# The feed-forward of a two-layer flow trunk: gate and up by seven products of halves, then the down product

## The chip, the cores and the metric

The kernel runs on one core of one Trainium2 chip. The metric is the device time of one execution in microseconds; of the kernel before three timed runs are shown, with a median of 3389.33 us (3386.82 to 3394.78).

## The reference

A trunk of two layers over 1024 latent tokens (`x`) with 256 context tokens (`ctx`), model width D = 1024, all in float32. A layer mixes tokens (gating, windowed attention, a recurrence) and then runs the feed-forward, which is the part that the change touches. Cut to that:

```python
D_FF = 2816                       # 22 blocks of 128

def swiglu(h, w_gu, w_down):
    gu = h @ w_gu                 # 1024 -> 2 * 2816: gate and up
    return (jax.nn.silu(gu[..., :D_FF]) * gu[..., D_FF:]) @ w_down

def trunk_layer(x, xc, c_act, cc_act, lp, last):
    sh1, sc1, gt1, sh2, sc2, gt2 = split(c_act @ lp['w_mod'] + lp['b_mod'], 6)   # modulations
    ...
    h = modulate(rms_norm(x, g[2]), sh2, sc2)
    x = x + gt2 * rms_norm(swiglu(h, lp['w_gu'], lp['w_down']), g[3])
    if last:
        return x, xc
    hc = modulate(rms_norm(xc, g[2]), mc[3], mc[4])
    xc = xc + mc[5] * rms_norm(swiglu(hc, lp['w_gu'], lp['w_down']), g[3])
```

So layer 0 sends 1024 latents and 256 context tokens through the feed-forward, layer 1 the 1024 latents alone.

## The kernel before

**Number format.** Products are made in three passes: each operand is split into hi (ScalarE copy to fp32r) and lo (VectorE, value minus hi), and `mm3` (L147) issues hi x hi, hi x lo and lo x hi into the same PSUM accumulator. All its matmuls stand in line L145. Weights come from DRAM in float32 as 128 x 1024 (512 KB) and are split on chip: `emit_w` loads into one of two buffers `wr` (L221), splits on ACT into `wh` (L229) and on DVE into `wl` (L230); `wh` and `wl` share six buffers. Which weights are loaded, and in which order, is the list `plan`, filled ahead; `wget` hands out the next pair and keeps two ready.

**Tokens.** They are in three groups `TG`: 0 = the 256 context columns, 1 and 2 = 512 latent columns each. The input of the feed-forward is transposed, `h2[z][k]`: z is hi or lo, k one of 8 blocks of 128 model columns, 1280 token columns in a slot. There are 33 such slots (`alloc`, `rel`); PSUM has accumulators `mm` (2 of one bank), `xx` (2 of one bank) and `dd` (2 of two banks).

**The feed-forward (from L1503).** For each block f of 128 hidden columns `gate_up(f)` runs `gu_group` for each token group: gate into the first bank of a `dd` accumulator, up into the second, each over 8 k. Then comes silu(gate) x up: tanh on ACT (L1518), two DVE operations (L1519, L1520), and the split of the result into `ah` (ACT, L1522) and `al` (DVE, L1523), which stay in slots. After each pair of f, `ffn_down` multiplies them by `w_down`: for each tile of 128 tokens and each half of 512 output columns a product of the two f into `mm` or `xx`, added by DVE to `yac`, the sum in SBUF (L1550):

```python
        ffn_down((0,), [wget()], True)
        gate_up(2)
        for q in range(NQ):
            ...
            gate_up(2 * q + 3, mq(0))
            ffn_down((2 * q + 1, 2 * q + 2), [wget(), wget()], False)
            gate_up(2 * q + 4, mq(1))
        gate_up(NFF - 1)
```

The first two f are interleaved with the norm that makes `h2`; the last call of `ffn_down` takes three f and calls `finish` for each tile: norm, residual and store. In layer 0, `mods_quarter` computes three of the modulations of layer 1 beside gate and up: 48 loads of `w_mod` into slots `wm`, two to a step, and 192 matmuls of 32 x 512. POOL has no work in the feed-forward.

Engines run their own instructions in the order in which the program issued them; they wait for one another through semaphores that the framework sets. All the loads and stores named here are issued by SP.

Of the kernel before, what the change touches and what calls it, by code (L numbers as in the profile page):

```python
# [17 lines left out]
L = 2  # L18
DM = 1024
# [16 lines left out]
FA = 6, 7, 8, 9  # L36
NP = 2
PPW = 111
C_DECAY = 0.3032653298563167
# [52 lines left out]
def trunk(ctx: ExitStack, tc: tile.TileContext, x, ctxt, cc, w_mod, pp, w_in, w_out, lng, lnb, sgw, sink,  # L92
# [50 lines left out]

    def mm(o, lhsT, rhs, start=True, stop=True):
        T.matmul(o, lhsT=lhsT, rhs=rhs, start=start, stop=stop)  # L145

    def mm3(o, a, b, start, stop):  # L147
        mm(o, a[0], b[0], start, False)
        mm(o, a[0], b[1], False, False)
        mm(o, a[1], b[0], False, stop)  # L150

# [83 lines left out]
    def wget(ahead=2, slots=False):  # L235
        if not ready:
            emit_w(slots)
        r = ready.popleft()
        while len(ready) < ahead and plan:
            emit_w(slots)  # L240
        return r
# [25 lines left out]

    NQ = (NFF - 4) // 2
    for k in range(8):
# [3 lines left out]
    for l in range(L):  # L273
        for n, i in enumerate(MIXT):
            plan_in(l, mix_col(i), 128)
            if l == 0:
                for _ in range(MODN[n]):
                    plan.extend(mblk.popleft())
        for c0 in (256, 0, OFF_CTX, OFF_Q, OFF_Q + 256):
            plan_in(l, c0, 256)  # L280
        for k in range(8):
            plan_rows(w_out[l], k)
        if l == 0:
            for k in range(8):
                plan.extend(mod_blocks(0, 2, k))
        plan_gu(l, 0)
        plan_gu(l, 1)
        plan_rows(w_down[l], 0)
        plan_gu(l, 2)
        for q in range(NQ):  # L290
            plan_gu(l, 2 * q + 3)
            if l + 1 < L and q < 6:
                for k in range(2):
                    plan.extend(mod_blocks(l + 1, q // 2, 4 * (q % 2) + k))
            plan_rows(w_down[l], 2 * q + 1)
            plan_rows(w_down[l], 2 * q + 2)
            plan_gu(l, 2 * q + 4)
            if l + 1 < L and q < 6:
                for k in range(2, 4):
                    plan.extend(mod_blocks(l + 1, q // 2, 4 * (q % 2) + k))  # L300
        plan_gu(l, NFF - 1)
        for f in range(NFF - 3, NFF):
            plan_rows(w_down[l], f)

# [12 lines left out]

    def mod_step(ps, k, start, stop):


        w = wget(), wget()
# [13 lines left out]

    def mods(l, qs, bank=d_t):

        for q in qs:
            ps = bank()
            for k in range(8):  # L340
                mod_step(ps, k, k == 0, k == 7)
# [8 lines left out]
    def mods_quarter(l, q, g, acc):  # L350

        ps = x_t()
        for k in (2 * g, 2 * g + 1):
            mod_step(ps, k, k == 2 * g, k == 2 * g + 1)
            yield
        for z in range(2):
            c = ps[:, z * 256:(z + 1) * 256]
            if g == 0:
                S.activation(acc[z], c, AF.Copy)
            else:  # L360
                V.tensor_tensor(acc[z], acc[z], c, op=ALU.add)
        yield
        if g == 3:
            mod_cols(l, q, x_t(), lambda kk: acc[kk // 2][:, (kk % 2) * 128:(kk % 2) * 128 + 128])

# [50 lines left out]

    def norm_apply(l, which, gi, xn, hT):

        c0, n = TG[gi]
        strm = 1 if gi == 0 else 0  # L420
        for k2 in range(4):
            tmp = alloc("ntmp")
            for kk in range(2):
                ps = x_t() if kk else mm_t()
                k = 2 * k2 + kk
                for j, s in enumerate(xn):
# [4 lines left out]
                             bias=AB[l][:, 2 * which + 1, 2 * k + strm:2 * k + strm + 1])  # L431
                hi, lo = hk(hT, k, c0, n)
                if kk:
# [5 lines left out]
            if k2 == 3:  # L439
                rel(*xn)  # L440
            yield

    def g_tiles(gi):
# [114 lines left out]
    def layer(l):  # L558
# [943 lines left out]
        rel(lora, *GB.values(), *Y)  # L1502
        h2 = hT_alloc()  # L1503


        act = {}

        def gu_group(gi, w, ah, al, tmp):
            c0, n = TG[gi]
            ps = d_t()  # L1510
            for z in range(2):
                for k in range(8):
                    mm3(ps[:, z * 512:z * 512 + n], (w[z][0][:, k * 128:(k + 1) * 128], w[z][1][:, k * 128:(k + 1) * 128]),
                        hk(h2, k, c0, n), k == 0, k == 7)
                    if k % 4 == 3:
                        yield
            tm = tmp.t[:, c0:c0 + n]
            S.activation(tm, ps[:, 0:n], AF.Tanh, scale=0.5)  # L1518
            V.scalar_tensor_tensor(tm, tm, 1.0, ps[:, 0:n], op0=ALU.add, op1=ALU.mult)  # L1519
            V.tensor_tensor(tm, tm, ps[:, 512:512 + n], op=ALU.mult)  # L1520
            hi = ah.t[:, c0:c0 + n]
            S.activation(hi, tm, AF.Copy, scale=0.5)  # L1522
            V.scalar_tensor_tensor(al.t[:, c0:c0 + n], tm, 0.5, hi.bitcast(F32), op0=ALU.mult, op1=ALU.subtract)  # L1523

        def gate_up(f, mg=None):
            w = wget(), wget()
            ah, al = alloc("ah", F32R), alloc("al", F32R)
            tmp = alloc("ft")
            n = 0
            for gi in gord:  # L1530
                for _ in gu_group(gi, w, ah, al, tmp):
                    n += 1
                    if mg and n in (2, 5, 7, 9):
                        next(mg, None)
            rel(tmp)
            act[f] = (ah, al)

        def ffn_down(fs, wd_, first, after=None, order=gord, side=iter(())):
            pend = []
            for t in [t for gi in order for t in g_tiles(gi)]:  # L1540
                for h in range(2):
                    c = slice(h * 512, (h + 1) * 512)
                    ps = mm_t() if h == 0 else x_t()
                    for j, f in enumerate(fs):
                        a = tuple(s.t[:, t * 128:(t + 1) * 128] for s in act[f])
                        mm3(ps, a, tuple(w[:, c] for w in wd_[j][:2]), j == 0, j == len(fs) - 1)
                    if first:
                        S.activation(yac[t].t[:, c], ps, AF.Copy)
                    else:
                        V.tensor_tensor(yac[t].t[:, c], yac[t].t[:, c], ps, op=ALU.add)  # L1550
                if after:
                    pend.append(after(t))
                    for g in list(pend):
                        if next(g, pend) is pend:
                            pend.remove(g)
                    next(side, None)
            for f in fs:
                rel(*act.pop(f))
            for g in pend:
                run(g)  # L1560
# [28 lines left out]
        ft = alloc("ft")  # L1589
        ff = []  # L1590

        def n2(gi):
            n2_load(gi)
            yield from norm_apply(l, 1, gi, [keep[t] for t in g_tiles(gi)], h2)

        def gu2(gi):
            for f in range(2):
                if gi == gord[0]:
                    ff.append((alloc("ah", F32R), alloc("al", F32R)))
                yield from gu_group(gi, wf[f], *ff[f], ft)  # L1600

        run(n2(gord[0]))
        for i, gi in enumerate(gord):
            weave(gu2(gi), n2(gord[i + 1]) if i + 1 < len(gord) else iter(()))
        for f in range(2):
            rel(*[z for w in wf[f] for z in w[2]])
            act[f] = ff[f]
        rel(ft)
        yac = {t: alloc("yac") for t in tiles_q}
        macc = [yac[t].t[:, DM:NTOK] for t in tiles_q[:2]]  # L1610
        ffn_down((0,), [wget()], True)
        gate_up(2)
        for q in range(NQ):
            def mq(z):
                return mods_quarter(l + 1, q // 2, 2 * (q % 2) + z, macc) if not last and q < 6 else None
            gate_up(2 * q + 3, mq(0))
            ffn_down((2 * q + 1, 2 * q + 2), [wget(), wget()], False)
            gate_up(2 * q + 4, mq(1))
        gate_up(NFF - 1)
        rel(*h2[0], *h2[1])  # L1620
        wd_ = [wget(0), wget(0), wget()]
        for strm in ([1, 0] if full else [0]):
            GB[strm] = gb_tile(l, 1, strm)
        if last:
            ffn_down(tuple(range(NFF - 3, NFF)), wd_, False, finish)
        else:
# [13 lines left out]

            ffn_down(tuple(range(NFF - 3, NFF)), wd_, False, finish, (2, 1, 0), norm_late())
            hT.append(h_slots())
# [74 lines left out]
```

## Time and profile before

| | |
|---|---|
| median of 3 timed runs | 3389.33 us (3386.82 to 3394.78) |
| profiled execution | 3392.51 us, span 3390.7 us |
| PE (matmul) | 3274.7 us, 97%, 20,348 records |
| DVE | 1787.4 us, 53%, 3,747 instructions |
| ACT | 1254.8 us, 37%, 2,735 |
| POOL | 330.9 us, 10%, 464 |
| mean DMA rate | 105 GB/s |
| PE on the chain that ended last | 21% of the span is named there, nearly all of it L145 |

A busy share is the engine's busy time over the span. It counts time in which the engine was at work, not time in which another had to wait for it; for that there are the chain of waits, the windows and the idle time before each group of instructions. The span is the time from the first to the last record of the profiled execution, which itself lasted 1.8 us longer.

### The profile page before, as it was taken

The numbers are of one execution on the slowest core, as the hardware profiler recorded it, in microseconds if no ns is written. First come the engines' busy times: TensorE is split into PE (matmuls) and PEld (weight loads), VectorE is DVE, ScalarE is ACT, GpSimd is POOL, SyncE is SP. The second block draws the span as 40 slices with busy tenths as digits, with TensorE's granted clock in tenths as the row PEclk, the third lists the DMA queues.
The fourth block names the chain that finished last, engine by engine and source line by source line (L and its number), as shares of the span: only waits on it lengthen the run. The fifth ranks groups of instructions, "written<-read, shape, count | busy, mean of one in ns | idle before, by whom it ended". The sixth has DMA issues, their size and how long they took to land. (4 is left out here: it accounts for less than half of the span.)

```text
span 3390.7 us, 51725 instructions
## 1 busy us (share of the span) xinstructions
PE 3274.7 (97%) x20348; PEld 2659.0 (78%) x20348; DVE 1787.4 (53%) x3747; ACT 1254.8 (37%) x2735; POOL 330.9 (10%) x464
## 2 busy tenths in 40 slices
PE   7998999999999999999999998999999999999998
PEld 4777877777787777778888777877777788888887
DVE  3458769775423333333334657788675433433445
ACT  4354477664431111111112554477664411111112
POOL 2103101231100000000000213111221000000000
PEclk8898999999999999999999999999999999999999
DMA  5684322446412222222112375423445111111113
GB/s 208 224 252 140 91 62 67 137 135 211 155 32 81 87 81 71 73 87 63 38 38 87 111 235 176 128 57 96 111 126 208 56 44 50 50 50 50 50 43 119
DMA packets 381778, 354.38 MB, mean 105 GB/s; under 512 B 111968, under 2 KB 332768, under 8 KB 381536
## 3 DMA queue, kind: packets, MB, share of 16 engines
q1 hardware_dynamic: 381536, 351.09, 32.9%
q8 instruction: 160, 2.62, 0.3%
q14 instruction: 82, 0.67, 0.1%
HBM read 255.20 MB, written 95.81 MB: 104 GB/s over the span
## 5 line engine op out<-in xcount | busy, mean ns | idle before, releaser
L145 PE MATMUL dd<-h,wh 128*128 128x512 f32 (+1 forms) x3440 | 983.7, 370 | 2.8 <-DVE h L437 2.7
L145 PEld LDWEIGHTS dd<-h,wh 128*128 128x128 f32 x3440 | 624.8, 189 | 140.7 <-issue 30.2
L145 PE MATMUL dd<-h,wl 128*128 128x512 f32 (+1 forms) x1720 | 634.5, 369 | 0.0
L229 ACT ACTIVATE wh<-wr 128x1024 fp32r<-128x1024 f32 x172 | 180.7, 1058 | 677.1 <-PE xx L145 367.0
L230 DVE TENSOR_TENSOR wl<-wr,wh 128x1024 fp32r<-128x1024 f32 x172 | 209.5, 1225 | 342.7 <-ACT wh L229 338.1
L145 PEld LDWEIGHTS dd<-h,wl 128*128 128x128 f32 x1720 | 325.0, 189 | 58.6 <-issue 5.0
L145 PE MATMUL mm<-wh,h 128*128 128x256 f32 x1472 | 327.6, 299 | 0.0
L1519 DVE SCALAR_TENSOR_TENSOR ft<-ft,dd 128x512 f32<-128x512 f32 (+1 forms) x110 | 69.5, 632 | 455.6 <-ACT ft L1518 455.6
L145 PEld LDWEIGHTS mm<-wh,h 128*128 128x128 f32 x1472 | 252.6, 197 | 15.6 <-issue 14.6
L1518 ACT ACTIVATE ft<-dd 128x512 f32<-128x512 f32 (+1 forms) x110 | 60.5, 550 | 497.7 <-PE dd L145 497.1
L145 PE MATMUL mm<-h,wh 128*128 128x512 f32 (+1 forms) x816 | 236.7, 375 | 1.0 <-ACT ntmp L429 0.7
L177 POOL TENSOR_TENSOR ss<-ss,mh_sb 128x1 f32<-128x1 f32 x74 | 49.9, 676 | 1830.8 <-DVE ss L406 1824.6
L145 PE MATMUL mm<-wl,h 128*128 128x256 f32 x736 | 213.7, 290 | 4.7 <-DVE wl L230 4.7
L145 PEld LDWEIGHTS mm<-h,wh 128*128 128x128 f32 x816 | 147.7, 196 | 34.7 <-issue 10.8
L1550 DVE TENSOR_TENSOR yac<-yac,mm 128x512 f32<-128x512 f32 x180 | 123.4, 686 | 86.9 <-PE mm L145 86.9
L1550 DVE TENSOR_TENSOR yac<-yac,xx 128x512 f32<-128x512 f32 x180 | 123.4, 686 | 84.7 <-PE xx L145 84.7
L145 PE MATMUL mm<-wh,ah 128*128 128x512 f32 x396 | 155.3, 392 | 2.1 <-DVE yac L1550 1.9
L145 PE MATMUL mm<-wh,al 128*128 128x512 f32 x396 | 154.7, 391 | 0.0
L145 PE MATMUL xx<-wh,ah 128*128 128x512 f32 x396 | 154.7, 391 | 0.0
L145 PE MATMUL mm<-wl,ah 128*128 128x512 f32 x396 | 154.6, 390 | 0.0
L145 PE MATMUL xx<-wl,ah 128*128 128x512 f32 x396 | 154.1, 389 | 0.0
L145 PE MATMUL xx<-wh,al 128*128 128x512 f32 x396 | 154.1, 389 | 0.0
(316 smaller groups left out, 5958.0 us busy)
## 6 DMA issues: line engine op xcount, KB each, us to landing
wr<-in_w_gu SPq DMA_DIRECT2D x88, 512.0 KB, 3.7
wm<-in_w_mod SPq DMA_DIRECT2D x80, 512.0 KB, 4.6
wr<-in_w_down SPq DMA_DIRECT2D x44, 512.0 KB, 3.3
wr<-in_w_in SPq DMA_DIRECT2D x38, 512.0 KB, 4.8
cb<-ao SPq DMA_DIRECT2D x76, 256.0 KB, 3.2
ao<-rk SPq DMA_DIRECT2D x58, 256.0 KB, 4.1
xs<-xr SPq DMA_DIRECT2D x28, 512.0 KB, 2.7
xr<-xs SPq DMA_DIRECT2D x26, 512.0 KB, 4.3
```

What stands on the lines that cost most here:

```text
L145: T.matmul(o, lhsT=lhsT, rhs=rhs, start=start, stop=stop)
L177: G.tensor_tensor(dst, src, mh[:, :n], op=ALU.pow)
L229: S.activation(hi, raw, AF.Copy)
L230: V.tensor_tensor(lo, raw, hi.bitcast(F32), op=ALU.subtract)
L1518: S.activation(tm, ps[:, 0:n], AF.Tanh, scale=0.5)
L1519: V.scalar_tensor_tensor(tm, tm, 1.0, ps[:, 0:n], op0=ALU.add, op1=ALU.mult)
L1550: V.tensor_tensor(yac[t].t[:, c], yac[t].t[:, c], ps, op=ALU.add)
```

## The change

The feed-forward is cut into two phases. In the first all activations are made and stored to DRAM as float32 (`actd`, 128 x 1280 for each f); in the second they are loaded again, split and multiplied by `w_down`.

**Phase 1.** f = 0, 1, 2 (`NCL` = 3) are computed as before (`gu_group`), with a store in the place of the split (L1511). For f = 3 to 21 gate and up of the latents are made together by one level of the Winograd form of Strassen's products. The weight block is a 2 x 2 array (gate, up by the two halves of k), the activations a 2 x 2 array (halves of k by halves of the columns; `h2k` lays the columns so that a half is 512 contiguous columns, 256 of each token group). Seven products of 4 k x 3 passes stand for eight. The sums of weights are made for each f by POOL in `prep` (L1565 to 1569), from `g` and `u`, loaded one f ahead; the four matrices g, u, a, b are split on ACT and DVE (L1575, L1576), two of them in `prep`, two at the start of the products (`w.late`). The sums of activations T1 to T4 are made once per layer, beside f = 0 to 2, by `t_sums` and `t_last` (DVE and ACT). `visit` makes one f. The context columns (layer 0) are computed as before, inside the visit.

```diff
+        def visit(f, w, tmp, aux):
+            a, c, d = mm_t(), x_t(), d_t()
+            b = d[:, 0:512]
...
+            p1, q = aux.t[:, 0:512], aux.t[:, 512:1024]
...
+            w.late[0]()
+            prod(1, a, True)
+            ctx(d[:, 512:768], 0, 0, True, False)
+            yield
+            S.activation(p1, a, AF.Copy)
+            prod(6, b, True)
+            yield
+            V.tensor_tensor(h2_, v(p1), v(b), op=ALU.add)
+            prod(5, c, True)
+            w.late[1]()
+            yield
+            V.tensor_tensor(q, p1, c, op=ALU.add)
+            prod(2, a, False, True)
+            ctx(d[:, 512:768], 0, 4, False, True)
+            yield
+            S.activation(h1, v(a), AF.Tanh, scale=0.5)
+            V.scalar_tensor_tensor(h1, h1, 1.0, v(a), op0=ALU.add, op1=ALU.mult)
+            prod(7, b, False)
+            yield
+            V.tensor_tensor(q, q, b, op=ALU.add)
+            prod(3, c, False, True)
+            yield
+            V.tensor_tensor(v(c), h2_, v(c), op=ALU.add)
+            ctx(d[:, 768:1024], 1, 0, True, False)
+            ctx(d[:, 768:1024], 1, 4, False, True)
+            prod(4, b, False, True)
+            silu(h2_, v(c), v(q))
+            yield
...
+            V.tensor_tensor(p1, p1, b, op=ALU.add)
+            V.tensor_tensor(h1, h1, v(p1), op=ALU.mult)
+            if f < NFF - 1:
+                lo = 0 if full else 256
+                D.dma_start(actd[f][:, lo:], tmp.t[:, lo:])
```

In it `prod` issues the 12 matmuls of one product, onto accumulator a (`mm`), b (first bank of a `dd`) or c (`xx`); `h1`, `h2_` are the halves of one slot `tmp`, which is then stored (L1649); `tmp` and `aux` are the same two slots for all f.

```diff
+        def prep(f, side, own):
...
+            for z, t in enumerate((g, u)):
+                D.dma_start(t.rearrange("p (a b) -> p a b", a=8), wv[:, :, z * DFF + f * 128:z * DFF + (f + 1) * 128])
+            yield
...
+            G.tensor_tensor(a[:, 0:512], u[:, 0:512], u[:, 512:1024], op=ALU.add)
+            G.tensor_tensor(a[:, 512:1024], a[:, 0:512], g[:, 0:512], op=ALU.subtract)
+            yield
+            G.tensor_tensor(b[:, 0:512], g[:, 0:512], u[:, 0:512], op=ALU.subtract)
+            G.tensor_tensor(b[:, 512:1024], g[:, 512:1024], a[:, 512:1024], op=ALU.subtract)
```

**Phase 2.** `ffn_down` runs over 8 groups of f, where there were 11 calls. Beside each group the next one's raw activations and rows of `w_down` are loaded (`act_load`, `wd_load`) and split (`act_split` on L1663 and L1664, `wd_split` on L1680 and L1681), one step for each token tile. The weights of every second group go to slots, those of the others to the six `wh` buffers. In layer 0 one step of the modulations of layer 1 (`mods` with `mget`, two loads ahead) stands beside each tile from the second group on; `mods_quarter` is gone.

```diff
+DOWN = [(0, 21), (1, 2, 3), (4, 5, 6), (7, 8, 9), (10, 11, 12), (13, 14, 15), (16, 17), (18, 19, 20)]
...
+        for i, fs in enumerate(DOWN[:-1]):
+            new = DOWN[i + 1]
+            slots = i % 2 == 1
...
+            def beside():
+                g = loads()
+                while True:
+                    next(g, None)
+                    if i:
+                        next(mg, None)
+                    yield
```

**On PE, in layer 1.** Before, a stretch of gate and up: `dd` is one accumulator for 24 matmuls, `h` are hi and lo of the activations, `wh` and `wl` those of the weights.

```order
L145 MATMUL dd_28397<-h_24627,wl_28208 128x512
L145 MATMUL dd_28397<-h_24628,wh_28207 128x512 x2
L145 MATMUL dd_28397<-h_24628,wl_28208 128x512
L145 MATMUL dd_28397<-h_24629,wh_28207 128x512 x2
L145 MATMUL dd_28397<-h_24629,wl_28208 128x512
L145 MATMUL dd_28397<-h_24622,wh_28213 128x512 x2
L145 MATMUL dd_28397<-h_24622,wl_28214 128x512
```

Now, the end of product 3 (onto c, `xx`) and the beginning of product 4 (onto b, `dd`) of one visit:

```order
L147 MATMUL xx_25967<-h_24702,wl_25970 128x512
L147 MATMUL xx_25967<-h_24703,wh_25969 128x512
L147 MATMUL xx_25967<-h_24711,wh_25969 128x512
L147 MATMUL xx_25967<-h_24703,wl_25970 128x512
L147 MATMUL dd_25968<-h_24696,wh_26019 128x512 [waits DVE_49,Activation_49]
L147 MATMUL dd_25968<-h_24704,wh_26019 128x512
L147 MATMUL dd_25968<-h_24696,wl_26020 128x512
```

An accumulator is now written by one product, read by DVE, and written by a later product of the same visit; product 4 waits for DVE's reading of b (L1634).

**On DVE, in layer 1.** Before, the end of one token group, two splits of weights and the end of the next:

```order
L1519 SCALAR_TENSOR_TENSOR ft_28219<-ft_28219,dd_28220 128x512 [waits Activation_49]
L1520 TENSOR_TENSOR ft_28219<-ft_28219,dd_28220 128x512 [waits DVE_49]
L1523 SCALAR_TENSOR_TENSOR al_28218<-ft_28219,ah_28217 128x512 [waits Activation_49]
L230 TENSOR_TENSOR wl_28214<-wr_28211,wh_28213 128x1024 [waits DMAHW3_49,PE_49,Activation_49]
L230 TENSOR_TENSOR wl_28331<-wr_28328,wh_28330 128x1024 [waits DMAHW4_49,PE_49,Activation_49]
L1519 SCALAR_TENSOR_TENSOR ft_28219<-ft_28219,dd_28274 128x512 [waits Activation_49]
```

Now, one visit whole, from the first addition after product 6 to the split that stands ahead of the next visit's (`ft` is `tmp`, `aux` holds p1 and q, `wu` and `wq` the weight matrices):

```order
L1622 TENSOR_TENSOR ft_24737<-aux_25335,dd_25842 128x2x256 [waits DMAHW6_49,PE_49,Activation_49]
L1626 TENSOR_TENSOR aux_25335<-aux_25335,xx_25841 128x512 [waits PE_49]
L1576 TENSOR_TENSOR wl_25894<-wu_25734,wh_25893 128x1024 [waits DMAHW1_49,Activation_49]
L1576 TENSOR_TENSOR wl_25913<-wq_25859,wh_25912 128x1024 [waits DMAHW5_49,PE_49,Activation_49]
L1631 SCALAR_TENSOR_TENSOR ft_24737<-ft_24737,mm_25840 128x2x256 [waits Activation_49]
L1634 TENSOR_TENSOR aux_25335<-aux_25335,dd_25842 128x512 [waits DVE_49,PE_49]
L1637 TENSOR_TENSOR xx_25841<-ft_24737,xx_25841 128x512 [waits PE_49]
L1576 TENSOR_TENSOR wl_25931<-wq_25876,wh_25930 128x1024 [waits Activation_49]
L1495 SCALAR_TENSOR_TENSOR ft_24737<-ft_24737,xx_25841 128x2x256 [waits Activation_49]
L1645 TENSOR_TENSOR aux_25335<-aux_25335,dd_25842 128x512 [waits PE_49]
L1496 TENSOR_TENSOR ft_24737<-ft_24737,aux_25335 128x2x256 [waits DVE_49]
L1646 TENSOR_TENSOR ft_24737<-ft_24737,aux_25335 128x2x256 [waits DVE_49]
```

Each f had four additions and multiplications, two splits of weights and two of activations; it now has nine of the first kind (one of them the first row) and four splits of weights. The first row waits for a DMA: the store of the f before, out of the same slot.

**On SP, in layer 1.** Before, two f of gate and up and a pair of down:

```order
L221 DMA wr_27047<-in_w_gu 128x8x128 [waits DMAHW6_49,DVE_49]
L221 DMA wr_27053<-in_w_gu 128x8x128 [waits DMAHW7_49,DVE_49]
L221 DMA wr_27170<-in_w_down 128x1024 [waits DMAHW0_49,DVE_49]
L221 DMA wr_27176<-in_w_down 128x1024 [waits DMAHW1_49,DVE_49]
L221 DMA wr_27293<-in_w_gu 128x8x128 [waits DMAHW2_49,DVE_49]
L221 DMA wr_27299<-in_w_gu 128x8x128 [waits DMAHW3_49,DVE_49]
```

Now, three visits:

```order
L1562 DMA wu_25860<-in_w_gu 128x8x128 [waits DMAHW6_49,DVE_49]
L1562 DMA wq_25859<-in_w_gu 128x8x128 [waits DMAHW2_49,DMAHW5_49,DVE_49,Pool_49]
L1649 DMA actd_24712<-ft_24737 128x1024 [waits DVE_49]
L1562 DMA wu_25986<-in_w_gu 128x8x128 [waits DMAHW1_49,DVE_49]
L1562 DMA wq_25985<-in_w_gu 128x8x128 [waits DMAHW0_49,DMAHW5_49,DVE_49,Pool_49]
L1649 DMA actd_24712<-ft_24737 128x1024 [waits DVE_49]
```

The loads of g (`wq`) and u (`wu`) for f + 1 stand between the store of f - 1 and that of f (L1649); a store waits for DVE's last multiplication (L1646), and the loads behind it wait with it.

## Rows read from the trace of the kernel before

**Rows 1.** Page: span, busy time and share by engine, GB/s in 40 slices.
```profile
span 3390.7 us, 51725 instructions
...
PE 3274.7 (97%) x20348; PEld 2659.0 (78%) x20348; DVE 1787.4 (53%) x3747; ACT 1254.8 (37%) x2735; POOL 330.9 (10%) x464
...
GB/s 208 224 252 140 91 62 67 137 135 211 155 32 81 87 81 71 73 87 63 38 38 87 111 235 176 128 57 96 111 126 208 56 44 50 50 50 50 50 43 119
```

**Rows 2.** Windows: feed-forward of layer 0, of layer 1, and two f there.
```profile
core 0: us, PE busy (x) PEld busy (x) DVE busy (x) ACT busy (x) POOL busy (x), PEclk, DMA share, GB/s
943.50:1676.90 733.40, 729.02 (x3555) 584.16 (x3553) 252.41 (x372) 120.88 (x181) 0.00 (x0) 1.00 0.23 70
2670.30:3344.70 674.40, 674.40 (x2978) 558.37 (x2977) 255.88 (x337) 124.58 (x165) 0.00 (x0) 1.00 0.17 53
2713.60:2757.20 43.60, 43.60 (x194) 36.08 (x194) 11.02 (x13) 8.37 (x13) 0.00 (x0) 1.00 0.16 48
```

**Rows 3.** Chain by time, layer 1: start us, us, engine, tile, line, count.
```profile
3170.77 43.52 PE dd L145 x192
3214.29 1.36 PE mm L145 x6
3215.65 1.36 PE xx L145 x6
```

**Rows 4.** Timeline of PE, layer 0: start us, us; context columns, then modulation.
```profile
start us, us, engine line op out<-in xcount [idle before <-releaser]
...
1108.64 0.28 PE L145 MATMUL dd<-h,wl 128*128 128x256 f32 x1
...
1111.52 0.28 PE L145 MATMUL dd<-h,wl 128*128 128x256 f32 x1
1112.52 1.05 PE L145 MATMUL xx<-wm,c 128*32 128x512 f32 x4 [0.72 <-DMA wm<-in_w_mod]
```

**Rows 5.** Groups of DVE and ACT, shapes apart: | busy us, mean ns |.
```profile
L230 DVE TENSOR_TENSOR wl<-wr,wh 128x1024 fp32r<-128x1024 f32 x172 | 209.5, 1225 | 342.7 <-ACT wh L229 338.1 <-PE mm L467 4.2 <-PE mm L145 0.4
...
L1550 DVE TENSOR_TENSOR yac<-yac,mm 128x512 f32<-128x512 f32 x180 | 123.4, 686 | 86.9 <-PE mm L145 86.9
...
L1523 DVE SCALAR_TENSOR_TENSOR al<-ft,ah 128x512 fp32r<-128x512 f32 x88 | 60.8, 691 | 47.9 <-ACT ah L1522 47.8
...
L1520 DVE TENSOR_TENSOR ft<-ft,dd 128x512 f32<-128x512 f32 x88 | 60.3, 685 | 2.3
...
L970 DVE TENSOR_TENSOR q<-mm,rope 128x256 f32<-128x256 f32 x32 | 13.4, 419 | 7.9 <-PE mm L145 7.5
...
L229 ACT ACTIVATE wh<-wr 128x1024 fp32r<-128x1024 f32 x172 | 180.7, 1058 | 677.1 <-PE xx L145 367.0 <-PE dd L145 269.7 <-PE mm L145 32.2
...
L1522 ACT ACTIVATE ah<-ft 128x512 fp32r<-128x512 f32 x88 | 55.6, 632 | 154.9 <-DVE ft L1520 154.9
...
L1518 ACT ACTIVATE ft<-dd 128x512 f32<-128x512 f32 x88 | 52.0, 591 | 387.5 <-PE dd L145 387.5
```

**Rows 6.** Groups of POOL, shapes apart: additions of 512 columns.
```profile
L437 POOL TENSOR_TENSOR h<-ntmp,h 128x512 fp32r<-128x512 f32 x16 | 21.7, 1358 | 58.2 <-DVE h L436 32.9 <-ACT h L434 16.0 <-ACT yt L400 5.7
...
L1326 POOL TENSOR_TENSOR gsx<-gsx,gkr 128x512 f32<-128x512 f32 x8 | 10.4, 1299 | 23.6 <-ACT gsx L1324 17.3 <-DMA gkr<-rk 6.3
```

**Rows 7.** Timeline of DVE and POOL, two places: start us, us.
```profile
922.20 1.29 POOL L437 TENSOR_TENSOR h<-ntmp,h 128x512 fp32r<-128x512 f32 x1 [9.35 <-DVE h L436]
922.21 1.82 DVE L437 TENSOR_TENSOR h<-ntmp,h 128x512 fp32r<-128x512 f32 x1
...
2546.84 1.28 POOL L1336 TENSOR_TENSOR Y<-Y,gsx 128x512 f32<-128x512 f32 x1 [6.70 <-DVE gsx L1335]
...
2547.03 2.16 DVE L230 TENSOR_TENSOR wsl<-wr,wsh 128x1024 fp32r<-128x1024 f32 x1
```

**Rows 8.** DMA issues: count, KB each, median us to landing.
```profile
wr<-in_w_gu SPq DMA_DIRECT2D x88, 512.0 KB, 3.7
...
wm<-in_w_mod SPq DMA_DIRECT2D x80, 512.0 KB, 4.6
...
wraw<-in_w_mod SPq DMA_DIRECT2D x16, 512.0 KB, 10.4
```

**Rows 9.** Line L1461, stores of 512 KB to DRAM.
```profile
DMA to landing us min/median/max: 2.6/2.8/5.1
```

**Rows 10.** Groups, layer 0: modulation matmuls, idle time and its releaser.
```profile
L145 PE MATMUL xx<-wm,c 128*32 128x512 f32 x192 | 44.3, 604 | 4.4 <-DMA wm<-in_w_mod 4.4
```

More of the change, by code (lines that the diff above doesn't have):

```diff
@@ L238, in wget @@
         r = ready.popleft()
-        while len(ready) < ahead and plan:
+        while len(ready) < ahead and plan and plan[0]:
             emit_w(slots)
@@ L285, in trunk @@
                 plan.extend(mod_blocks(0, 2, k))
[L286 to L303, printed above, removed]
+        for f in range(NCL):
+            plan_gu(l, f)
+        plan.append(None)
     S.activation(sc_, CC, AF.Tanh, scale=0.5)
@@ L1517, in gu_group @@
             tm = tmp.t[:, c0:c0 + n]
[L1518 to L1536, printed above, removed]
@@ L1539, in ffn_down, with wd_split @@
+        def wd_split(w):
+            hi, lo, own, raw = w
+            S.activation(hi, raw, AF.Copy)
+            V.tensor_tensor(lo, raw, f32(hi), op=ALU.subtract)
+        def ffn_down(fs, wd_, first, after=None, order=None, side=iter(())):
             pend = []
-            for t in [t for gi in order for t in g_tiles(gi)]:
+            for t in order:
                 for h in range(2):
@@ L1619, in layer, with both, sums @@
-        gate_up(NFF - 1)
-        rel(*h2[0], *h2[1])
-        wd_ = [wget(0), wget(0), wget()]
+                yield from gu_group(f, gi, wf[f], ft)
+        def both(*gs):
+            for g in gs:
+                yield from g
+        def sums(gi, kks):
+            for kk in kks:
+                if kk not in TT:
+                    TT[kk] = [alloc("tt", F32R) for _ in range(3)]
+                    if kk % 2 == 0:
+                        T4[kk // 2] = alloc("t4")
+                yield from t_sums(gi, kk)
@@ new lines, in layer, with plain @@
+        run(n2(gord[0]))
+        for i, gi in enumerate(gord[:-2]):
+            weave(gu2(gi), n2(gord[i + 1]))
+        ga, gb = gord[-2:]
+        weave(gu2(ga), both(n2(gb), sums(ga, (0, 1))))
+        side = []
+        more = [(wget(0), wget(0)) for _ in range(2, NCL)]
+        own = []
+        nxt = prep(NCL, side, own)
+        def plain(f):
+            w = more.pop(0)
+            for gi in gord:
+                yield from gu_group(f, gi, w, ft)
+            rel(*[z for x in w for z in x[2]])
@@ new lines, in after_two @@
+        def after_two():
+            yield from gu2(gb)
+            for f in range(2):
+                rel(*[z for w in wf[f] for z in w[2]])
+            for f in range(2, NCL):
+                yield from plain(f)
+        weave(after_two(), both(sums(gb, (0, 1)), sums(ga, (2,)), sums(gb, (2,)), sums(ga, (3,)), sums(gb, (3,))))
+        for kk in range(4):
+            t_last(kk)
+        own += [alloc("wq") for _ in range(3)]
+        run(nxt)
+        tmp, aux = ft, alloc("aux")
+        wd = {}
@@ new lines, in layer @@
+        for f in range(NCL, NFF):
+            w = side.pop()
+            if f < NFF - 1:
+                nxt = prep(f + 1, side, own)
+                for _ in visit(f, w, tmp, aux):
+                    next(nxt, None)
+                run(nxt)
+            else:
+                wd[0] = wd_load(0, False)
+                raw = None
+                for n, _ in enumerate(visit(f, w, tmp, aux)):
+                    if n == 1:
+                        rel(*own)
+                        raw = act_load(0)
+                        act_split(0, raw)
+                        rel(raw)
+                    if n == 3:
+                        wd_split(wd[0])
+                        wd[f] = wd_load(f, False)
+                    if n == 5:
+                        wd_split(wd[f])
@@ new lines, in layer @@
+        rel(aux, *h2[0], *h2[1], *[s for z in TT.values() for s in z])
+        if full:
+            act_split(NFF - 1, tmp, lambda ap: ap[:, 0:256])
+        for h in (1, 0):
+            act_split(NFF - 1, tmp, lambda ap: ap[:, 256 - lo_q:].rearrange("p (g h t) -> p g h t", g=2, h=2)[:, :, h])
+        rel(tmp)
+        yac = {t: alloc("yac") for t in tiles_q}
+        mw = deque()
+        mplan = deque(b for q in range(3) for k in range(8) for b in mod_blocks(l + 1, q, k)) if not last else deque()
@@ L1622, in layer @@
+        run(mg)
+        fs = DOWN[-1]
+        wd_ = [wd[f] for f in fs]
+        plan.popleft()
+        if plan:
+            for _ in range(2):
+                emit_w()
         for strm in ([1, 0] if full else [0]):
@@ L1624, in layer @@
         if last:
-            ffn_down(tuple(range(NFF - 3, NFF)), wd_, False, finish)
+            ffn_down(fs, wd_, False, finish, [t for gi in gord for t in g_tiles(gi)])
         else:
```

222 lines of the change are left out of this document (168 added, 54 removed).

## The prediction

> **What bounds the kernel now.** Read first the page's busy shares: PE is busy 97% of the span, DVE half of it, the others less [rows 1]. A busy share doesn't say that PE is the limit, so the second view is a table of windows: through the two feed-forward stretches (943.5 to 1676.9 us in layer 0, 2670.3 to 3344.7 in layer 1) PE has no gap in layer 1 and 4.4 us in layer 0, while DVE is busy for about a third, ACT for a sixth and POOL not at all; the granted clock is 1.00, the 2.4 GHz level, in both [rows 2]. The third view is the chain that ended last, in order of time: there the stretch is PE alone, 192 matmuls of gate and up in 43.52 us, then products of down, 6 in 1.36 us, again and again [rows 3]. That gives the price of the whole prediction: 43.52/192 = 1.36/6 = 0.2267 us for a matmul of 512 columns, for gate, up and down alike. (The 0.39 us of a single one in the timeline is its length from issue to end; they overlap.) The 256 columns of the context cost 2.88 us for 24, so 0.12 us each [rows 4]. Here time is the number of matmuls, and nothing else is on the path.
>
> The sum is made against the profiled execution, 3392.5 us (span 3390.7 and 1.8 around it). It lies 3.2 us above the median of the three timed runs, 3389.3, so the forecast is moved down by that at the end.
>
> **Matmuls removed.** For 19 of 22 blocks f, gate and up over the latents took 2 operands x 8 k x 3 passes x 2 token groups = 96 matmuls; now it is 7 products x 4 k x 3 passes = 84. 12 x 19 x 2 layers = 456 fewer, which is what the two orders count (8544 and 8088 of 512 columns; every other width is unchanged). 456 x 0.2267 = **103.4 us less**, if PE still waits for nothing. What remains is to ask at each place who is late next.
>
> **A visit of one f (19 per layer).** In layer 1 its 84 matmuls are 84 x 0.2267 = 19.0 us; in layer 0 the context adds 48 x 0.12 to make 24.8 us. Beside it DVE has nine operations of 512 at 0.69 us and four splits of 1024 at 1.23 us, together 11.1 us; ACT four splits at 1.06, one copy and two tanh at 0.59, together 6.0 us [rows 5]; POOL, idle here before, four additions at 1.36 us, 5.4 us [rows 6]. All fit under 19.0. Being in order matters more than the sums, so follow the waits in the new orders. The shortest is the second use of accumulator b: product 4 writes it again after DVE has added it to q (L1634). Only product 3 stands between, 12 x 0.2267 = 2.72 us, against 0.69 us of DVE and at most one split of 1.23 ahead of it in the queue: covered. The splits for the next f wait for buffers: that of a (needed by product 6 of the next visit) is released by product 3, costs 1.06 + 1.23 = 2.3 us, and has products 4 and 1, 5.4 us, as cover. The loads of gate and up for f + 1 stand on SP behind the store of f - 1, which DVE releases 2 to 3 us into the visit of f; they land some 3.7 us later [rows 8], at 7 us at the latest, and their first reader, the split of g, stands behind product 2, at 10.9 us. POOL's 5.4 us then end at 12.4, ahead of the split of a behind product 3, at 16.3.
>
> The longest chain goes round from visit to visit, because tmp and aux are single: after product 4, three DVE operations (2.1 us), the store to DRAM (512 KB; the nearest rows land in 2.8 us, at most 5.1 [rows 9]), then the first addition of the next visit, 0.69. With one split of 1.23 between, that is 6.8 us, at worst 9.1. Who waits for it is product 7, 4 x 2.72 = 10.9 us later in layer 1 and 13.8 in layer 0. Covered; I cost the visits at nothing.
>
> **Before the visits.** The sums T1 to T4 take, for each of 8 pairs of group and k, two additions of 512, four of 256 at 0.42 and two splits, about 4.2 us of DVE, 33 us in all [rows 5]. They stand beside gate and up of f = 0 to 2, 288 matmuls or 65 us in layer 1, in which DVE's old work was a quarter [rows 2]. The splitting of the activations (L1522, L1523) leaves this place for the down phase. Nothing on the path; if that cover failed the last pair would cost its 4.2 us per layer.
>
> **The down phase.** As many matmuls as before, in 8 groups instead of 11. Of a group of three f in layer 1 (144 matmuls, 32.6 us) DVE has 16 accumulations at 0.69, three splits of 1024 and three of the activations, each twice L1523's 0.69 at layer 1's 1024 columns: 19 us [rows 5]. Two seams are new. From the last visit to the first group: behind product 4 stand three DVE operations, one ACT copy (0.63) and one split (0.69), 3.4 us, against 12 matmuls with f = 0 that the order places ahead, 2.72 us. From group (0, 21) to (1, 2, 3): only six split buffers exist and four are held, so two weights are split after the last matmul, 2.3 us for the first against some 1.5 to 2 us of matmuls ready. I take 1 us for each seam, **4 us more** in the two layers; the bounds are 0 and 4 x 3.4 = 14.
>
> The 24 steps of the modulation product move from beside gate and up to beside down. Four matmul records take 1.05 us now [rows 4], and all 192 of them wait 4.4 us for their loads in total [rows 10]. Down issues one step per tile, 4.1 us of matmuls, against 4.6 us to land [rows 8]: if the loads were only one tile ahead that would be 24 x 0.5 = 12 us, but the order has SP one to two tiles further ahead. Zero taken, bounds -4 and +12.
>
> **Sum:** 3392.5 - 103.4 + 4 = 3293.1, less 3.2 for the median: **3290 us**, 3.0% faster.
>
> **Rivals.** (1) *DVE and POOL hinder one another.* Twice the timeline shows what that costs: a DVE subtraction of 512 beside a POOL one took 1.82 us instead of 0.69, a split of 1024 2.16 instead of 1.23 [rows 7]. In the chain round the visits three such operations (two multiplications with both inputs in SBUF, one split) can meet POOL's four additions, 3 x 1.1 = 3.3 us more. With stores at 2.8 us the chain is then 10.1 and still under 10.9; with every store at its worst 5.1 us it is 12.4, so 1.5 us late in each of layer 1's 19 visits, 28 us: 3318. For it: POOL's additions are new here. Against: they are free to run when the loads have landed, mostly before that chain. The Trainium skill (SBUF — State Buffer, Who interferes with whom) speaks against the change here: a VectorE instruction with two inputs in SBUF and a GpSimd instruction that reads SBUF exclude one another for a whole instruction. Rows 7 agree with it, 1.82 us being near the sum of the two; by that rule alone DVE's 11.1 us would become 16.5, still under the visit's 19.0.
>
> (2) *Down waits for loads.* The 12 us above, with both seams at their bound: about 3312. Against it, 1.05 MB per step of 6.1 us and about 3.5 MB per group are some 230 GB/s, and a slice near the start already moved 252 [rows 1].
>
> (3) *Slower than before.* The mechanism is the store inside the chain round the visits: 99 us of gain over 38 visits are eaten when each is 2.6 us late. With rival 1's 3.3 us in full that takes stores landing in 6.2 us in layer 1 and 7.9 in layer 0 (there the context's two DVE operations of 0.42 and its tanh add 1.2 to the chain). If they landed as the most crowded loads of the trace do, 10.4 us [rows 8], product 7 would wait 6.8 us in each of 19 visits and 5.1 in the others, 226 us: some 3510. Against it: in these windows the DMA engines are busy a fifth of the time [rows 2], and no store of this size took over 5.1.
>
> (4) *The saving is not made*, because the seven products cost PE more than their columns: 0.2267 us holds here for two different operand patterns [rows 3], and the orders show the 456 gone, so I give that little.
>
> **How the numbers follow.** The forecast has 0.72 (3290, by itself 3280 to 3305: bounds of the seams, the modulation loads, and the 4 us of gaps that layer 0 may lose). Rival 1 in part or full 0.13, rival 2 0.09, rival 3 0.02, rival 4 or a lower clock 0.04 (between 3330 and 3400). The range that should hold 8 in 10 is 3281 to 3317. A measurement here tells 0.2%, 7 us, from no change: faster 0.96, the same 0.01, slower 0.03.
>
> **What would show it.** In the changed profile PE should show some 456 records fewer than 20,348 [rows 1] (a few may be missing), a visit in layer 1 should last 19.0 us and one in layer 0 24.8, with PE free of gaps; POOL should be busy some 200 us more. PE idle before products onto dd, released by DVE L1634 or L1622, would be rivals 1 and 3; idle before the matmuls on wm, or L1680 and L1663 as releasers, rival 2. Visits of more than 20 us in layer 1, or a stretch of down longer than its matmuls x 0.2267 us by more than 10, would make the prediction wrong.

## The result, and the profile after

The changed kernel took 3274.69 us (median of 4 runs, 3271.0 to 3277.66), the kernel before in the same comparison 3390.77; the ratio is 0.9657 (0.964 to 0.9674). It is 3.4% faster, where 3.0% were forecast: 116 us instead of 99, and 15.3 us below the predicted 3290, outside the stated range. The profiled execution lasted 3271.0 us, 22 less than the sum had for it (3293.1).

The page after, span and busy time, against [rows 1]:

```profile
span 3269.2 us, 51898 instructions
...
PE 3153.1 (96%) x19892; PEld 2568.1 (79%) x19892; DVE 2038.0 (62%) x3978; ACT 1349.4 (41%) x2805; POOL 538.5 (16%) x616
```

PE has 456 records fewer, just the matmuls removed, and POOL 208 us more. The windows answer to [rows 2], for phase 1 alone: the visits of layer 0 with the gate and up that stand ahead of them, one visit there, the same stretch of layer 1, and one of its visits:

```profile
core 0: us, PE busy (x) PEld busy (x) DVE busy (x) ACT busy (x) POOL busy (x), PEclk, DMA share, GB/s
938.50:1470.70 532.20, 532.20 (x2796) 459.31 (x2795) 293.67 (x363) 137.63 (x184) 103.87 (x76) 1.00 0.22 74
1026.23:1051.09 24.86, 24.86 (x134) 21.51 (x134) 13.39 (x16) 6.19 (x8) 5.46 (x5) 1.00 0.21 69
2599.10:3014.70 415.60, 415.60 (x1835) 344.10 (x1835) 265.70 (x325) 130.50 (x165) 103.71 (x76) 1.00 0.26 85
2748.94:2767.98 19.04, 19.04 (x86) 15.77 (x85) 11.85 (x14) 5.81 (x8) 5.45 (x5) 1.00 0.26 83
```

PE has no gap in either stretch; a visit lasts 24.86 and 19.04 us, as forecast (24.8 and 19.0). So the products are not where the forecast failed. To find the place, cut the span at marks that both traces have: in each layer one usual step behind the start of the output projection's last matmul (`dd` from `mhi`), and the start of the last matmul of down.

| us | before | after | difference | forecast |
|---|---|---|---|---|
| layer 0, end of the output projection to last matmul of down | 990.7 | 918.1 | -72.6 | -49.7 |
| layer 1, the same | 732.3 | 686.1 | -46.2 | -49.7 |
| all the rest, code that the change leaves alone | 1667.8 | 1665.1 | -2.7 | 0 |

The difference lies in layer 0, which alone has the modulations of layer 1 beside its feed-forward. Their group there, after, against [rows 10]:

```profile
L147 PE MATMUL dd<-wm,c 128*32 128x512 f32 x192 | 29.7, 604 | 0.3 <-DMA wm<-in_w_mod 0.3
```

The same 192 records take 29.7 us of PE in place of 44.3, and wait 0.3 us in place of 4.4. The timeline of PE says why. First after, then a place of the kernel before that [rows 4] did not include (modulations of layer 0 beside its output projection):

```profile
1532.89 0.39 PE L147 MATMUL xx<-wh,al 128*128 128x512 f32 x1
1533.21 1.06 PE L147 MATMUL dd<-wm,c 128*32 128x512 f32 x8
1534.21 0.50 PE L147 MATMUL mm<-wh,ah 128*128 128x512 f32 x1
```

```profile
879.30 1.06 PE L145 MATMUL mm<-wm,c 128*32 128x512 f32 x8
880.29 0.50 PE L145 MATMUL dd<-wh,mhi 128*128 128x512 f32 x1
```

A matmul of the modulations leaves two records, so the 192 records are 96 matmuls, and not the 192 that the description of the kernel has. Eight records, the four matmuls of a step, take 1.06 us when they stand together; in [rows 4] four records, two matmuls, took 1.05. Each of a step's four matmuls writes 32 output rows of its own, and they run beside one another. The Trainium skill (TensorEngine Tiling (Array Packing), Tiling Modes) lists four independent tiles for this shape and says that different tiles can execute in parallel; these rows agree. In the order of the kernel before a step was mostly torn apart, since its two weight blocks come by two loads, and each pair waits for its own:

```
L145 MATMUL xx_10647<-wm_10615,c_94 32x512 [waits DMAHW2_49]
L145 MATMUL xx_10647<-wm_10615,c_94 32x512
L145 MATMUL dd_10622<-h_9758,wh_10446 128x256
...
L145 MATMUL dd_10622<-h_9759,wl_10441 128x256
L145 MATMUL xx_10647<-wm_10617,c_94 32x512 [waits DMAHW3_49]
```

(The dots stand for four of the six matmuls between.) The description of the kernel before puts these loads into slots, which is wrong: there they share the six buffers of `wh` and `wl`. In the change they have slots of their own, and by its order a step's second pair mostly stands with the next step's first. Counted in the traces, layer 0's feed-forward has 42 groups before and 25 after. A group that waits for nothing lengthens PE's time by 1.2 us whether it is of four records or eight. From the start of the last ordinary matmul before a group to the start of the second behind it, less their usual steps, the groups cost 55.6 us before (waits included) and 34.3 after, 21.3 less. In six places before, a single matmul stands between two groups and its delay is counted with both; counted once, the sums are 54.5 and 34.5, 20.0 less. With 228 matmuls x 0.2267 = 51.7 that makes 71.7 to 73.0, where layer 0 gained 72.6.

### The profile page after: what moved, and what is told of

Its sections match the earlier page's. It is cut to its first block, busy times and chain, and to the rows that moved or that the text cites. A ratio compares the mean times of both kernels' runs of the same rounds, so it can differ in the third digit from the quotient of the medians.

```text
span 3269.2 us, 51898 instructions
## 1 busy us (share of the span) xinstructions
PE 3153.1 (96%) x19892; PEld 2568.1 (79%) x19892; DVE 2038.0 (62%) x3978; ACT 1349.4 (41%) x2805; POOL 538.5 (16%) x616
## 4 chain that ended last, share of the span: by engine, by line
PE 80%; DVE 8%; DMA 3%; issue 3%; ACT 3%; POOL 2%; SPq 1%; DVEq 0%; POOLq 0%; ACTq 0%
PE dd L147 26%; PE mm L147 24%; PE xx L147 18%; PE u L147 7%; PE mm L1118 1%; DMA wraw<-in_w_mod 1%; PE gg L147 1%; PE uy L147 1%; PE xx L1118 1%; DVE eX L666 1%; DVE eL L664 1%; DVE P L1071 1%; POOL ss L179 0%; DMA wm<-in_w_mod 0%; DVE yac L1697 0%
## 5 line engine op out<-in xcount | busy, mean ns | idle before, releaser
L147 PE MATMUL mm<-h,wh 128*128 128x512 f32 (+1 forms) x1424 | 424.2, 382 | 2.9 <-ACT ntmp L399 2.3
L147 PE MATMUL dd<-h,wh 128*128 128x256 f32 (+1 forms) x1312 | 321.8, 336 | 1.5 <-DVE h L407 1.0
L147 PE MATMUL mm<-h,wl 128*128 128x512 f32 (+1 forms) x712 | 268.5, 377 | 1.1 <-DVE wl L232 1.1
L147 PEld LDWEIGHTS dd<-h,wh 128*128 128x128 f32 x1312 | 228.0, 191 | 29.2 <-DVE h L407 1.2
L1575 ACT ACTIVATE wh<-wq 128x1024 fp32r<-128x1024 f32 x114 | 121.0, 1061 | 302.8 <-PE dd L147 113.9
L147 PE MATMUL dd<-h,wl 128*128 128x256 f32 (+1 forms) x656 | 219.3, 334 | 0.0
L1576 DVE TENSOR_TENSOR wl<-wq,wh 128x1024 fp32r<-128x1024 f32 x114 | 141.1, 1238 | 114.8 <-ACT wh L1575 114.8
L147 PE MATMUL dd<-tt,wh 128*128 128x512 f32 x608 | 188.1, 391 | 0.0
L147 PEld LDWEIGHTS mm<-h,wl 128*128 128x128 f32 x712 | 136.8, 192 | 25.3 <-DVE wl L232 1.4
L147 PEld LDWEIGHTS mm<-wl,h 128*128 128x128 f32 x736 | 145.0, 197 | 7.4 <-DVE wl L232 4.7
L1565 POOL TENSOR_TENSOR wq<-wu 128x512 f32<-128x512 f32 x38 | 49.1, 1292 | 561.8 <-DVE wl L1576 477.8
L147 PEld LDWEIGHTS dd<-h,wl 128*128 128x128 f32 x656 | 124.9, 190 | 12.4
L147 PEld LDWEIGHTS dd<-tt,wh 128*128 128x128 f32 x608 | 111.7, 188 | 21.3
```

Source lines behind the costliest of these rows:

```text
L147: T.matmul(o, lhsT=lhsT, rhs=rhs, start=start, stop=stop, skip_group_check=parts)
L1565: G.tensor_tensor(a[:, 0:512], u[:, 0:512], u[:, 512:1024], op=ALU.add)
L1575: S.activation(w.hi[i], raw[i], AF.Copy)
L1576: V.tensor_tensor(w.lo[i], raw[i], f32(w.hi[i]), op=ALU.subtract)
```

## Experiments

Each was compared with the kernel before. The two runs on the modulations, the one with two phases and the one with one f fewer ran on one chip; the other four, the change itself among them, on a second.

**The modulations torn apart in the change.** Instead of `mods`, a loop that issues two matmuls beside one token tile and two beside the next:

```diff
-        mg = mods(l + 1, (0, 1, 2), d_t, mget) if not last else iter(())
+        def mods_halves():
...
+                    for z in range(2):
+                        wm = mget()
+                        for j in (2 * z, 2 * z + 1):
+                            mm(ps[32 * j:32 * j + 32, 0:512], C48[:, 2 * k:2 * k + 32], wm[0][:, ...], k == 0, k == 7)
+                        rel(wm[1])
+                        if 2 * k + z < 15:
+                            yield
...
+        mg = mods_halves() if not last else iter(())
```

> The changed kernel, with each modulation step of layer 1 cut in two: two matmuls beside one token tile of down, two beside the next, so that the order has 44 groups of modulation matmuls there where the change has 25. Theory (a group of two matmuls costs PE what a group of four costs, 1.2 us): 19 groups more x 1.2 = 23 us slower than the change, 3298 us (3294 to 3303). Rival (the 20 us that layer 0 gained beyond the 456 matmuls came from loads that no longer hold PE up, 4.4 us, or from elsewhere): within 5 us of the change, 3271 to 3280.

Measured: 3299.18 us (3297.44 to 3303.01), ratio 0.9727 (0.9714 to 0.974), so 24.5 slower than the change by the medians, near the theory's 23. Layer 0's feed-forward lasts 937.8 us in place of 918.1, layer 1's 687.3. Of these 19.7 us in layer 0 the groups make 19.1: counted as above, they cost 53.4 in place of 34.3. The rest of the 24.5 lies in other stretches and was not followed up. The modulations' row, and one pair:

```profile
L147 PE MATMUL dd<-wm,c 128*32 128x512 f32 x192 | 46.4, 605 | 0.0
```

```profile
1541.45 1.05 PE L147 MATMUL dd<-wm,c 128*32 128x512 f32 x4
1542.43 0.50 PE L147 MATMUL mm<-wh,ah 128*128 128x512 f32 x1
```

46.4 us without any wait for a load: the price is the number of groups, and not the loads.

**The modulations kept together in the kernel before.** They stay beside gate and up, with no products of halves and in one phase; the loads go to slots, issued some matmuls ahead. For this the steps stand beside every second f, and two or three of them, not two, share an accumulator, which the expectation does not mention:

```diff
...
+        for k in ks:
+            w = []
+            for src, _, _ in mod_blocks(l, q, k):
+                w.append(alloc("wm"))
+                D.dma_start(w[-1].t[:, :1024], src)
+            yield
+            for j in range(4):
+                mm(ps[32 * j:32 * j + 32, 0:512], C48[:, 2 * k:2 * k + 32], w[j // 2].t[:, ...], k == ks[0], k == ks[-1])
+            rel(*w)
```

> The kernel before, with the modulations of layer 1 still beside gate and up, but the two loads of a step issued some matmuls ahead into slots of their own, so that its four matmuls stand together: 24 groups where the kernel before has 42. Nothing else is changed, there are no Strassen products and one phase. Theory: 42 groups cost 55.6 us there (waits included), 24 x 1.2 = 28.8 now, so 27 us faster than before: 3364 us (3360 to 3369). Rival (only the waits for loads go): 4 us faster, 3386.

Measured: 3366.52 us (3364.4 to 3367.33), ratio 0.9923 (0.9909 to 0.9937), 24.8 us faster than before by the medians. Layer 0's feed-forward fell from 990.7 to 963.8, by 26.9, the 27 of the theory; layer 1's is 732.3 as before. PE's own stream has the gain: counted as above, the 24 groups cost 28.7 us in place of 55.6.

```profile
L145 PE MATMUL xx<-wm,c 128*32 128x512 f32 x192 | 25.6, 605 | 0.0
```

The two runs settle the cause from both sides: some 20 us of the change's gain belong to the way the modulations' matmuls are grouped, and as much can be had without a single Strassen product.

**Two phases, all products classical.** 

```diff
-NCL = 3
+NCL = NFF
...
+        for f in range(2, NFF - 1):
+            run(plain(f))
...
+        for gi in gord:
+            act_split(NFF - 1, ft, lambda ap: ap[:, TG[gi][0] - lo_q:TG[gi][0] + TG[gi][1] - lo_q])
```

> The changed kernel without its seven products: all 22 f by the eight classical products, still in two phases through DRAM, with the modulations beside down. Theory (the products save their columns and nothing more): 456 x 0.2267 = 103 us slower than the change, 3378 us (3374 to 3383), that is 13 us faster than before, which is the modulations' 21 less the seams and the entry of layer 1. Rival (the two phases alone change nothing and the products saved all 116 us): 3391, as before.

Measured: 3385.61 us (3382.33 to 3396.7), ratio 0.9984 (0.9974 to 0.9993), 7.6 above the theory and outside its range, 5 below the rival. Layer 0 gives what was expected: 968.4, so 22.3 less than before and 50.3 more than the change (51.7 for 228 matmuls). Layer 1 lasts 743.8, which is 57.7 more than the change. Most of these 6 us too many arise at this kernel's own seam to down. PE waits 4.2 us there for ACT's split of the last f (its values are there at 3128.0), which stands in ACT's order behind the split of another f, and that one waits 3.86 us for its activations to come back from DRAM. The stretch right behind runs at a granted clock of 0.50, the 1.2 GHz level:

```profile
3129.60 1.06 ACT L1663 ACTIVATE ah<-ar 128x1024 fp32r<-128x1024 f32 x1 [3.86 <-DMA ar<-actd]
3130.56 0.61 ACT L1663 ACTIVATE ah<-ft 128x512 fp32r<-128x512 f32 x1
```

```profile
3131.30:3135.00 3.70, 3.70 (x9) 2.96 (x10) 2.35 (x3) 1.20 (x2) 0.00 (x0) 0.50 0.53 172
```

Each matmul's excess over 0.2267 us, summed over 3120 to 3140 us, makes 7.1 us lost, against 1.7 at that seam in the change. By its total the run doesn't tell the products from this; the next one does.

**Seven products from f = 12 on.** Entry, last visit and down stay.

```diff
-NCL = 3
+NCL = 12
...
-        more = [(wget(0), wget(0)) for _ in range(2, NCL)]
+        more = [(wget(0), wget(0))]
...
-            w = more.pop(0)
+            w = more.pop(0) if more else (wget(), wget())
```

> The change with seven products from f = 12 on instead of 3; entry, last visit and down phase stay as in the change. Theory (a product is worth its columns, 0.2267 us a matmul, and the visits wait for nothing): 9 f x 12 matmuls x 2 layers x 0.2267 = 49.0 us slower than the change, 3324 us (3320 to 3328). Rival (the comparison with two classical phases showed 111 us for 19 f, 5.8 each, and that is the products'): 52.6 us, 3327; the two are told apart in the profile, by the stretch of f = 3 to 11: 9 x 96 x 0.2267 = 195.9 us in layer 1, without gaps, against 9 x 19.04 = 171.4 in the change.

Measured: 3331.89 us (3327.85 to 3335.78), 55.0 above the run of the change beside it (3276.85); ratio 0.9826 (0.981 to 0.9843). The chain in layer 1, through f = 3 to 11:

```profile
2632.50 250.03 PE dd L147 x1103
```

250.03/1103 = 0.2267 without a gap, so a classical f costs 96 x 0.2267 = 21.76 us against 19.04 of a visit. The two layers' feed-forwards are 22.1 and 27.8 us longer than in that run, 49.9 together where 49.0 were expected; against the change's first profile they are 26.1 and 27.5 longer, so the sums alone don't tell theory from rival, and the chain without a gap has to. 5 of the remaining us lie in layer 1's token mixing, whose code is the same. A product is worth its columns, and no more.

**One f fewer ahead of the visits.**

```diff
-NCL = 3
+NCL = 2
```

> The change with one more f by seven products (from f = 2 on instead of 3): 24 matmuls fewer over both layers, 5.4 us, with a third less work to cover the activation sums. Theory (the sums stay covered, as 1.4 us of idle PE in the two entries of the change suggest): 3270 us (3267 to 3273). Rival (the last two pairs of sums, 4.2 us of VectorE each, and the last splits now hold up product 6): 2 x (8.4 - 2.7) = 11 us slower than the change, 3286.

Measured: 3303.18 us (3302.14 to 3312.09), 28 slower than the change: the rival's direction, and worse than its 11. The first product of the first visit, layer 1:

```profile
2665.34 0.68 DVE L1536 TENSOR_TENSOR tt<-tx,tt 128x512 fp32r<-128x512 f32 x1
...
2666.16 1.78 POOL L1565 TENSOR_TENSOR wq<-wu 128x512 f32<-128x512 f32 x1 [41.52 <-issue]
2667.09 1.06 ACT L1575 ACTIVATE wh<-wq 128x1024 fp32r<-128x1024 f32 x1 [1.00 <-DMA wq<-in_w_gu]
...
2668.18 4.41 DVE L1576 TENSOR_TENSOR wl<-wq,wh 128x1024 fp32r<-128x1024 f32 x2 [1.36 <-ACT wh L1575]
...
2668.20 1.22 PE L147 MATMUL mm<-h,wh 128*128 128x512 f32 x2 [10.59 <-ACT wh L1575]
```

PE stands still for 10.6 us in both layers, and for product 1, which needs no sum at all: the weights' load and split stand behind the sums of the activations. SP held this load of `wq` back 2.8 us for a split of the sums (L1536) and issued it at 2663.46; it landed 3.6 us later. Behind the wait the granted clock is 0.50:

```profile
2668.00:2675.00 7.00, 5.79 (x13) 4.10 (x14) 4.52 (x3) 2.26 (x3) 6.90 (x4) 0.50 0.02 5
```

The third f is cover that is needed.

**The change again.**

> The changed kernel once more, on the chip of the next three. Every theory: 3275 us (3270 to 3280). The stretch ahead of layer 0's output projection, whose code the change does not touch, lasted 776.7 to 783.6 us in six profiles; it should again fall there, so that the 3.9 us which the change's first profile gained in it are no effect of the change.

Measured: 3276.85 us (3270.23 to 3277.87). The stretch ahead of layer 0's output projection lasted 779.8 us, within the 776.7 to 783.6 of the six profiles before it, so what the change's first profile gained there is no effect of the change. Layer 0's feed-forward lasted 922.1, of which 2.05 us one wait for `wm`, layer 1's 685.8. Over ten profiles the code outside the feed-forward took 1665 to 1678 us.

**The weight sums on VectorE.** The four additions of `prep` issued by `V` instead of `G`.

> The change with the four weight sums of each visit on VectorE instead of POOL. Theory (VectorE has room: 11.1 us of work in a visit of 19.04 become 13.9, and product 7's wait for the store has 4.3 us of slack): the same within 5 us, 3275; and the multiplication on L1646, 1.77 us beside POOL, falls back to 0.69. Rival (in order behind the sums, the reading of accumulator b on L1634 comes late for product 4, whose cover is 2.7 us): 1 us late in each of 38 visits, 38 us slower, 3313.

Measured: 3278.96 us (3276.29 to 3284.61), the two feed-forwards 918.6 and 686.7: the same. The multiplication on L1646 over all visits (ns, min/median/max), of the change and of this kernel:

```profile
L1646 DVE TENSOR_TENSOR ft<-ft,aux x38: 684/1762/1775, 1027.1 to 3016.3; 128x512 f32<-128x512 f32 x38
```

```profile
L1646 DVE TENSOR_TENSOR ft<-ft,aux x38: 684/687/694, 1028.8 to 3022.9; 128x512 f32<-128x512 f32 x38
```

So POOL does hold DVE up, by 1.1 us in every visit, and it costs nothing.

**No POOL in layer 1's second norm.**

```diff
-                (G if k % 3 == 2 else V).tensor_tensor(lo, tm, hi.bitcast(F32), op=ALU.subtract)
+                (G if k % 3 == 2 and not (l == L - 1 and which) else V).tensor_tensor(lo, tm, hi.bitcast(F32), op=ALU.subtract)
```

> The change with the few subtractions that POOL makes in layer 1's second norm (L408, two or three of 512 columns for each token group) on VectorE. Theory (layer 1's entry lost 3.5 us because a VectorE scaling of 1024 columns took 1.75 us beside POOL's subtraction instead of 0.74, and the statistics on POOL stood behind it): the gap of 2.15 us goes, layer 1's feed-forward lasts 2 to 4 us less than 686.1, the total 3272. Rival (the entry is bound by VectorE's own work): layer 1 the same or up to 2 us longer, 3275 to 3277.

Measured: 3272.04 us (3268.62 to 3275.44), ratio 0.965 (0.9635 to 0.9664). By the total it can't be told from the change; by the profile layer 1's feed-forward lasts 683.0 us in place of 686.1 and 685.8. The scaling in the change, and here:

```profile
2582.19 1.26 POOL L408 TENSOR_TENSOR h<-ntmp,h 128x512 fp32r<-128x512 f32 x1
2582.26 1.75 DVE L385 TENSOR_SCALAR yt<-xr,ss 128x1024 f32<-128x1024 f32 x1 [0.44 <-POOL ss L179]
...
2584.06 0.18 PEld L397 LDWEIGHTS mm<-cst_sb,yt 128*128 128x128 f32 x1 [2.34 <-DVE yt L385]
```

```profile
2582.46 0.75 DVE L385 TENSOR_SCALAR yt<-xr,ss 128x1024 f32<-128x1024 f32 x1 [0.44 <-POOL ss L179]
...
2583.26 0.14 PEld L397 LDWEIGHTS mm<-cst_sb,yt 128*128 128x128 f32 x1 [0.19 <-DVE yt L385]
```

Here DVE is on PE's path: with POOL out of the way the wait of PE's weight load for DVE falls from 2.34 to 0.19 us.

## Why the prediction was wrong, step by step

- **Matmuls removed:** right. 456 records fewer, 0.2267 us each, 51.7 us per layer.
- **Visits at nothing:** right. The chain round the visits, in layer 1:

```profile
2749.13 0.80 DVE L1496 TENSOR_TENSOR ft<-ft,aux 128x512 f32<-128x512 f32 x1
...
2749.45 1.62 POOL L1566 TENSOR_TENSOR wq<-wq,wq 128x512 f32<-128x512 f32 x1
...
2749.85 1.77 DVE L1646 TENSOR_TENSOR ft<-ft,aux 128x512 f32<-128x512 f32 x1
...
2751.55 1.21 DVE L1576 TENSOR_TENSOR wl<-wq,wh 128x1024 fp32r<-128x1024 f32 x1
...
2751.65 0.34 SPq L1649 DMA_DIRECT2D actd<-ft  x1
...
2754.36 0.69 DVE L1622 TENSOR_TENSOR ft<-aux,dd 128x512 f32<-128x512 f32 x1 [1.60 <-DMA actd<-ft]
...
2758.85 0.37 SPq L1562 DMA_DIRECT2D wu<-in_w_gu  x1
...
2759.20 0.62 PE L147 MATMUL dd<-tt,wh 128*128 128x512 f32 x2
```

  The store lands 2.7 us after its issue, L1622 ends at 2755.05, and product 7 starts at 2759.20: 4.1 us of slack, as worked out (10.9 - 6.8). That the sum fits to 0.1 us is luck: the split of 1.23 that it has in the chain stands behind the last multiplication and runs beside the store (L1576), and rival 1's 1.2 us stand in its place. Rival 1's mechanism is there, at 1.2 us (1.08 on L1646, 0.11 on L1496) in place of 3.3, and is covered; rival 3's stores took 4.0 us at most. The rule that the prediction took from the Trainium skill (SBUF — State Buffer, Who interferes with whom) agrees with L1646, which took 1.77 us and ended 0.55 us after POOL's L1566.
- **Loads:** a slip without effect. POOL sums the weights of f + 1 at the very start of the visit of f (L1566 above), so these were loaded in the visit before, and the load at 2758.85, half way into the visit, is that of f + 2. The loads stand one f further ahead than in the prediction and in the description of the change, and are issued some 8 to 11 us earlier than the prediction had them.
- **Sums ahead of the visits:** right that they are covered; the run with one f fewer shows that little is to spare.
- **Seams:** 2 us per layer taken. At the first, PE waited 0.88 us in layer 0 and 1.38 in layer 1; at the second no gap over 0.3 us shows. With the slower matmuls behind the wait the first cost 1.7 us in layer 1, about what was taken.
- **The modulations are the step that failed:** "Zero taken, bounds -4 and +12". It was -20 to -21. The step asked only whether the loads would come in time, and took the matmuls' own price as fixed at 1.05 us for four records (a step of eight stands at 2.1 us in rival 2's 6.1), though the trace of before had eight records for 1.06 us elsewhere. A look at how the two orders group them would have given (42 - 25) x 1.2 = 20 us; 3290 - 20 is within 5 us of the measured median.
- **Left out:** the entry of layer 1, the stretch of the second norm. Each matmul's excess over its usual step, summed from the output projection to the first steady product, makes 9.5 us against 6.0 before: 3.5 us, which is what layer 1 fell short of its forecast. PE's wait for the scaling beside POOL is in it, and the granted clock of the stretch behind, after and before (first row and second):

```profile
2584.00:2591.00 7.00, 6.94 (x28) 5.84 (x28) 6.96 (x13) 3.15 (x5) 1.34 (x1) 0.79 0.00 0
```

```profile
2659.00:2666.00 7.00, 6.72 (x33) 5.33 (x34) 4.72 (x9) 3.49 (x6) 1.30 (x1) 1.00 0.00 1
```

  The run without POOL in that norm won back 2.8 to 3.1 us, so POOL's subtractions are the cause of most of it. Why POOL's subtraction meets that scaling only in the change was not tried.

The range was too narrow on the fast side for the same reason: its lower bound let the modulations gain no more than their waits, 4.4 us.

## What to carry to other kernels

When work is moved, price it again at its new place: what stands next to an instruction is part of its price, above all for small matmuls that run beside one another, whose cost went here by groups and not by instructions. Compare the groups in the two orders as carefully as the instructions removed. A big change's gain should be split by stage before it is put down to its idea: here about a sixth of it came from where a side product landed, and could have been had alone.

## What the runs showed of the hardware

- Two matmuls of 32 output rows (four records) cost 1.05 us, four that stand together 1.06; cut apart, the same 192 records took 46.4 us of PE, together 25.6. Between ordinary matmuls a group of either size lengthened PE's time by 1.2 us.
- A DVE multiplication of 512 columns with both inputs in SBUF took 1.77 us beside a POOL addition and 0.69 without one; a scaling of 1024 columns 1.75 and 0.75. In the kernel with one f fewer two splits of 1024 took 4.41 us beside POOL, in place of 2 x 1.23.
- In two kernels a long wait of PE in an otherwise full stretch was followed by a granted clock of 0.50: a wait of 4.2 us by 0.50 over the 3.7 us read, one of 10.6 us by 0.50 over 7 us.
